# Two plain pairs of steps instead of three in both FFNs, with earlier squares and two low parts by accumulating DMA

## The chip, the cores and the metric

The kernel runs on one core of one Trainium2 chip. A core has a matrix engine (TensorE, PE in the profile; PEld is its weight loading), a vector engine (VectorE, DVE), a scalar engine (ScalarE, ACT), a general one (GpSimd, POOL) and a synchronising engine (SyncE, SP); each runs its own list of instructions in order and waits on semaphores for the others. DMA transfers are issued by an engine (here SP and POOL) and land later. The metric is the device time of one execution in microseconds (us).

## The reference

One sequence of 512 tokens with 1024 features goes through two layers, in fp32. Layer 0 is a dilated window attention, layer 1 an mLSTM; behind each stands a feed-forward network (FFN), and a final norm ends it. The change is in the two FFNs and in the norms ahead of them:

```python
def swiglu(xn, w_in, w_out):
    gu = xn @ w_in
    return (jax.nn.silu(gu[..., :D_FF]) * gu[..., D_FF:]) @ w_out
...
    for i in range(DEPTH):
        ...                       # h = h + mixer(rms_norm(h, ...))
        h = h + swiglu(rms_norm(h, ffn_norm[i]), ffn_w_in[i], ffn_w_out[i])
    return rms_norm(h, final_norm)
```

D_FF is 2816, so `w_in` is 1024x5632 per layer: the gate half and the up half.

## The kernel before, in words

Features lie on the 128 partitions, tokens along the free dimension: the residual stream is eight tiles h0 to h7 of 128x512. A product in fp32 precision is made of three matmuls in a shorter format (fp32r): each operand is split into a high part, a copy that ACT rounds, and a low part, the rest, which DVE subtracts; high by high, high by low and low by high are added up in PSUM (`SPLITS`, line 42). `split_chunk` (line 204) does this for a chunk of weights (128x1024, three buffers each for raw, high and low, `W_BUFS`), `split_act` and `x_tiles` for activations.

Ahead of an FFN, `norm` (line 828) splits h, scaled by the norm's gains, and makes the sum of squares: ACT squares each h tile, DVE adds it to `ssum`. PE sums over the partitions (tile n1ss in FFN 0, n3ss in FFN 1), DVE takes the reciprocal root, and `hook` (line 327) has PE spread it to all partitions, from where DVE copies it into `rbc`. The FFN's first matmuls don't wait for it: they multiply the unnormalised tokens, and `rbc` is applied to their result. The norm of FFN 0 (n1) stands behind the attention's output projection (`out_project`, tiles awo), which adds its result to h two tiles at a time; that of FFN 1 (n3) behind the mLSTM's (tiles mwo).

`ffn_in` (line 860) makes the hidden layer in 11 pairs of steps: pair j (j = 0, 2, ... 20) yields two blocks of 128 hidden features. The first PLAIN // 2 pairs, three here (`PLAIN`, line 857), are plain (`plain`, line 943): 96 matmuls of 128x512 through `multiply` (line 240), tiles f0j and f1j. At the end of a pair DVE multiplies four accumulators by `rbc` (tiles gu, line 959) and makes the hidden values (hid, line 964).

The other eight pairs use a scheme of seven products instead of eight (Strassen's, in Winograd's form). The weights of a pair are seen as blocks A11, A12, A21, A22 (half: gate or up; part: which 512 features of the input), the normalised tokens as B11, B12, B21, B22 (512 features by 256 tokens), and seven products of sums of them (`PRODUCTS`, S1 to S4 and T1 to T4) give the result. Each product is 24 matmuls of 128x256 (line 1017). The order is A11·B11, S1·T1, S2·T2, A12·B21, S3·T3, S4·B22, A22·T4; `products` (line 1005) writes them and reads their results, `weights_of` (line 970) loads the four blocks by SP (line 980), makes the sums S by DVE (line 988) and splits them, `AHEAD` = 2 products ahead.

The token operands are made once per FFN by the generator `normalized` (line 894), a few steps at a time beside the plain pairs: eight normalised tiles (f0x or f1x, line 900) into two buffers with the tag w8, x0 and x1 (x0 holds B11 and B12, x1 holds B21 and B22); T1 into a buffer with the tag t1 (tile f0t or f1t); T3 over B12, T2 over B22, T4 over B21. `split_tokens` (line 888) splits each of the seven into a high part (ACT, line 891) and a low part (DVE, line 892). The buffers are used again: the raw blocks A11 and A21 of the first seven-product pair go into x0's place, those of the second into x1's, and the sums S1, S2 of the first into t1's. So a first A11 load has to wait until all readers of B11, B12 and T3 are done, and the first S until those of T1 are.

In FFN 1, `residual` (line 1660) also turns h, two passes of transposes by DVE (hB) and transfers by POOL (hD) to device memory and back, for the natural token order at the end; in FFN 0 sums of hidden tiles (tile f0S) and of rows of the output weights (accumulating DMAs by POOL, line 1138) are made beside the pairs for the output stage, `output_products` (line 1090).

The order of each engine's instructions is fixed at build time: the statements are put in order by a scheduler that looks at dependences and buffers, so that an engine's list can differ from the order of the lines; it doesn't change at run time.

Of the kernel before, what the change touches and what calls it, by code (L numbers as in the profile page):

```python
# [11 lines left out]
F32 = mybir.dt.float32  # L12
F32R = mybir.dt.float32r
I32 = mybir.dt.int32
AF = mybir.ActivationFunctionType
ALU = mybir.AluOpType
AX = mybir.AxisListType
P = 128

SEQ = 512  # L20
D = 1024
KC = D // P
# [49 lines left out]
def tile_hybrid_dilated_attn_mlstm(  # L72
# [4 lines left out]
    nc = tc.nc  # L77
# [3 lines left out]
    def pool(stack, name, **kw):  # L81
        return stack.enter_context(tc.tile_pool(name=name, bufs=1, **kw))
# [147 lines left out]
    def x_tiles(name):  # L230
        parts = [xp.tile([P, 2, SEQ], F32R, tag="x%d" % i, name="%s_%s%d" % (name, "hl"[i % 2], i // 2))
                 for i in range(KC)]
        return [[parts[k // 2 * 2 + part][:, k % 2] for k in range(KC)] for part in range(2)]
# [11 lines left out]
    def project(pairs, w2d, c0, nk, evac, name, hook=None, ready=()):  # L245

        acc = [acc_tile("%s_%d" % (name, m)) for m in range(2)]
        for ch in range((nk + 3) // 4):
            n = min(4, nk - 4 * ch)
            whl = ready.pop(0) if ready else split_chunk(weight_chunk(w2d, ch, c0, n, "%s_k%d" % (name, ch)))  # L250
            for m in range(2):
                with fenced():
                    multiply(acc[m], whl, pairs, ch, m, nk)
                if 4 * ch + n == nk and hook is None:
                    evac(m, acc[m])
            if 4 * ch + n == nk and hook is not None:
                hook()
                for m in range(2):
                    evac(m, acc[m])
            advance()  # L260
# [81 lines left out]
    hp = pool(ctx, "h")  # L342
    npl = pool(ctx, "norm")
    h = [hp.tile([P, SEQ], F32, tag="h", name="h%d" % k, bufs=KC + 1) for k in range(KC)]

    with ExitStack() as actx:
        ap = pool(actx, "attn")
# [59 lines left out]
        pair = x_tiles("xa")  # L407
# [92 lines left out]
        rbc, rtok, bc_hook = inverse_rms(v, "x", box, then=lambda bp: rope_scale(bp))  # L500
# [28 lines left out]
        def rope_scale(bp):  # L529
            nc.vector.tensor_tensor(sinr, bp[:R], sinn, op=ALU.mult)  # L530
            nc.vector.tensor_tensor(rbc[:R], bp[:R], cosn, op=ALU.mult)
# [253 lines left out]
        pair = x_tiles("ao")  # L785
# [3 lines left out]
        def add_to_h(c):  # L789
            def evac(m, acc):  # L790
                nc.vector.tensor_tensor(h[2 * c + m], acc, h[2 * c + m], op=ALU.add)
            return evac

        def out_project(pairs, w2d, nk, name, first=0, end=KC // 2):
            for c in range(first, end):
                project(pairs, w2d, c * 256, nk, add_to_h(c), "%s%d" % (name, c))
# [7 lines left out]
        def out_part(c, whl, ch, ks=None, last=False):  # L804
            for m in range(2):
                with fenced():
                    multiply(acc[c][m], whl, pair, ch, m, KC, ks)
                if last:
                    add_to_h(c)(m, acc[c][m])
# [12 lines left out]
        for k in range(2, 4):  # L822
            for c in range(3):
                out_part(c, whl[c], 1, (k,), k == 3)
    out_project(pair, attn_w_out[0], KC, "awo", first=3)


    def norm(key, k0, name):
        pair = x_tiles(name)
        ssum = npl.tile([P, SEQ], F32, tag="ssum", name=name + "ssum")  # L830
        for k in range(KC):
            split_act(pair[0][k], pair[1][k], h[k], col(key, k0 + k))
            if k == 0:
                nc.scalar.activation(ssum, h[k], AF.Square)
            else:
                sq = npl.tile([P, SEQ], F32, tag="sq", name=name + "sq", bufs=2)
                nc.scalar.activation(sq, h[k], AF.Square)
                nc.vector.tensor_tensor(ssum, ssum, sq, op=ALU.add)
        v = npl.tile([P, TB], F32, tag="rs_v4", name=name + "v", bufs=2)
        box = {}  # L840

        def sums():
            sp = ps.tile([P, 512], F32, tag="t", name=name + "ss", bufs=1)
            for tb in range(TB):
                nc.tensor.matmul(sp[:, tb:tb + 1], ssum[:, tb * P:(tb + 1) * P], ones[:, 0:1],
                                 start=True, stop=True)
            nc.vector.tensor_copy(v, sp[:, :TB])
            box["finish"]()
        rbc, r, hook = inverse_rms(v, name, box)
        defer(1, sums)  # L850
        return pair, rbc, r, hook
# [2 lines left out]
    HALF = SEQ // 2  # L854

    PRODUCTS = (("A11", "B11"), ("S1", "T1"), ("S2", "T2"), ("A12", "B21"), ("S3", "T3"), ("S4", "B22"), ("A22", "T4"))
    PLAIN = 6
    AHEAD = 2

    def ffn_in(layer, fp, pair, rbc, hook, following, hid, during):  # L860
# [24 lines left out]

        ops, raw = {}, {}

        def split_tokens(key):
            i = [b for _, b in PRODUCTS].index(key)
            hi, lo = ops[key] = [op_tile(2 * i + part, key + "hl"[part]) for part in range(2)]  # L890
            nc.scalar.activation(hi, raw[key], AF.Copy)
            nc.vector.tensor_tensor(lo, raw[key], hi.bitcast(F32), op=ALU.subtract)

        def normalized():
            xs = [fp.tile([P, 4, SEQ], F32, tag="w8", name="f%dx%d" % (layer, i), bufs=2) for i in range(2)]
            for i in range(2):
                for t in range(2):
                    raw["B%d%d" % (i + 1, t + 1)] = xs[i][:, :, t * HALF:(t + 1) * HALF]
            for k in range(KC):
                nc.vector.scalar_tensor_tensor(xs[k // 4][:, k % 4], h[k], col("ffn", layer * KC + k), rbc,  # L900
                                               op0=ALU.mult, op1=ALU.mult)
                yield
            split_tokens("B11")
            raw["T1"] = fp.tile([P, 4, HALF], F32, tag="t1", name="f%dt1" % layer)
            nc.vector.tensor_tensor(raw["T1"], raw["B12"], raw["B11"], op=ALU.subtract)
            yield

            raw["T3"] = raw["B12"]
            nc.vector.tensor_tensor(raw["T3"], raw["B22"], raw["B12"], op=ALU.subtract)
            split_tokens("T1")  # L910
            yield
            split_tokens("T3")
            yield
            split_tokens("B22")
            yield
            raw["T2"] = raw["B22"]
            nc.vector.tensor_tensor(raw["T2"], raw["B22"], raw["T1"], op=ALU.subtract)
            split_tokens("T2")
            yield
            split_tokens("B21")  # L920
            yield

            raw["T4"] = raw["B21"]
            nc.vector.tensor_tensor(raw["T4"], raw["B21"], raw["T2"], op=ALU.subtract)
            split_tokens("T4")
# [4 lines left out]
        def some(n):  # L930
            for _ in itertools.islice(steps, n):
                pass


        chunks = [(j, ch, half) for j in range(0, PLAIN, 2) for ch in range(KC // 4) for half in range(2)]
        ready = []
# [126 lines left out]
        split_next()  # L1063
        for j in range(0, PLAIN, 2):
            plain(j)
        todo = [(j, i) for j in range(PLAIN, FC, 2) for i in range(len(PRODUCTS))]
        prepared = {}

        def prepare(n):
            if n < len(todo):  # L1070
                j, i = todo[n]
                if j not in prepared:
                    prepared[j] = weights_of(j)
                prepared[j][0][i]()
            else:
                following(n - len(todo))

        for n in range(AHEAD):
            prepare(n)
        some(None)  # L1080
        for n, (j, i) in enumerate(todo):
            prepare(n + AHEAD)
            if i == 0:
                steps_of = products(j, prepared[j][1])
            steps_of[i]()
            if i % 2:
                advance()
            during(j, i)
# [207 lines left out]
            return [(kind, ops[(a, b) if kind == "product" else b], whl[a, b]) for kind, a, b in items[-TAIL:]]  # L1296
        return hid, during, prepare, work

    pair, rbc, _, hook = norm("ffn", 0, "n1")
    with ExitStack() as fctx:  # L1300
        fp = pool(fctx, "ffn0")
        hid, during, prepare, work = output_products(0, fp, ffn_w_out[0], True)
# [24 lines left out]
        old, h = h, []  # L1327
# [26 lines left out]


    pair, rbc, rtok, hook = norm("mlstm", 0, "n2")
    w_in2 = mlstm_w_in[0]
    with ExitStack() as mctx:
# [138 lines left out]
        i = 0  # L1497
# [136 lines left out]
        ypair = x_tiles("yo")  # L1634
# [10 lines left out]
        run_deferred()  # L1645
        for j in range(H):
            split_act(ypair[0][j], ypair[1][j], y[j], hg[:, j:j + 1])
    out_project(ypair, mlstm_w_out[0], KC, "mwo")


    pair, rbc, _, hook = norm("ffn", KC, "n3")
    with ExitStack() as fctx:
        fp = pool(fctx, "ffn1")
        dp = pool(fctx, "scratch1", space=bass.MemoryType.DRAM)
# [11 lines left out]
                                    t[R * a_:R * (a_ + 1)])  # L1666

        def during(j, i):
            if i == 3:
                residual(((j - PLAIN) // 2 + 4) % KC)  # L1670
            operands(j, i)
        ffn_in(1, fp, pair, rbc, hook, prepare, hid, during)
# [131 lines left out]
```

## Time and profile before

| | us |
|---|---|
| median of 3 runs | 1409.27 |
| runs, lowest to highest | 1408.67 to 1409.78 |
| profiled execution, time | 1408.68 |
| profiled execution, span (first to last instruction) | 1406.9 |
| PE busy | 1394.5 |
| DVE busy | 1054.9 |
| ACT busy | 665.4 |
| POOL busy | 149.0 |

The times in the rows are counted from the span's start; FFN 0's first matmul starts at 503.20. A row of the timeline gives start and duration in us, engine, line, operation, and which tile is written from which; x2 stands for two such instructions in a row, and a bracket holds the idle time before it and what ended it. A duration includes time in which the next instruction of the engine has started, so the distance of two starts is the cost of one in a full queue.

### The profile page before, as it was taken

Reading aid. Unit: us, or ns where it says so; the run is one execution under the profiler, and the core shown is the slowest. Engines: PE = TensorE matmul, PEld = TensorE weight load, DVE = VectorE, ACT = ScalarE, POOL = GpSimd, SP = SyncE. Lnnn points to the kernel's source line nnn. Section 1 sums busy time; section 2 is a strip of 40 time slices with the busy share of each in tenths; the row PEclk is TensorE's granted clock in tenths of the full one; section 3 lists DMA queues with packets and bytes.
Section 4 is the critical chain, followed back from the end, with each engine's and each line's share of the span. In section 5 each row is a group of like instructions: output and inputs, shape, how many; then the busy total and the mean of one; then the engine's idle time right before and its main releaser. Section 6 shows DMA issues by size and latency. Waiting matters only on the chain. (4 is left out here: it accounts for less than half of the span.)

```text
span 1406.9 us, 21243 instructions
## 1 busy us (share of the span) xinstructions
PE 1394.5 (99%) x8226; PEld 1237.5 (88%) x8226; DVE 1054.9 (75%) x1832; ACT 665.4 (47%) x1111; POOL 149.0 (11%) x222
## 2 busy tenths in 40 slices
PE   9999999999999999999999999999999999999998
PEld 7888888888888888999999998888888899999886
DVE  7866557566567298777877898998758888887875
ACT  5333224224225253444576463786534444458744
POOL 1011011002002000000000101113101240001111
PEclk9999999999999999999999999999999999999999
DMA  6346245335434455433263733234333553335861
GB/s 195 102 109 203 76 117 160 118 106 131 159 105 121 157 143 156 106 120 119 68 180 85 161 110 103 82 89 106 96 100 105 168 158 117 120 102 125 174 192 60
DMA packets 137277, 176.02 MB, mean 125 GB/s; under 512 B 8596, under 2 KB 111316, under 8 KB 137176
## 3 DMA queue, kind: packets, MB, share of 16 engines
q1 hardware_dynamic: 121392, 134.17, 30.8%
q0 software_dynamic: 14128, 39.37, 12.5%
q8 instruction: 64, 1.05, 0.3%
q10 hardware_dynamic: 1656, 1.12, 0.2%
q14 instruction: 37, 0.30, 0.1%
HBM read 158.91 MB, written 15.73 MB: 124 GB/s over the span
## 5 line engine op out<-in xcount | busy, mean ns | idle before, releaser
L240 PE MATMUL f0j<-n_h,f0j_h 128*128 128x512 f32 x96 | 37.5, 390 | 0.0
L240 PE MATMUL f1j<-n_h,f1j_h 128*128 128x512 f32 x96 | 37.5, 390 | 0.0
L240 PE MATMUL f0j<-n_h,f0j_l 128*128 128x512 f32 x96 | 37.4, 389 | 0.0
L240 PE MATMUL f1j<-n_h,f1j_l 128*128 128x512 f32 x96 | 37.4, 389 | 0.0
L240 PE MATMUL f0j<-n_l,f0j_h 128*128 128x512 f32 x96 | 37.3, 389 | 0.0
L240 PE MATMUL f1j<-n_l,f1j_h 128*128 128x512 f32 x96 | 37.3, 389 | 0.0
L1138 POOL DMA_DIRECT2D f0S<-in_ffn_w_out_dram x10 | 8.7, 866 | 265.1 <-ACT f0P L1120 155.1
L1163 POOL DMA_DIRECT2D f1T<-in_ffn_w_out_dram x12 | 14.6, 1217 | 179.0 <-ACT f1T L1166 151.6
L1665 POOL DMA_DIRECT2D hD<-hB x32 | 20.7, 653 | 96.4 <-DVE hB L1662 96.4
L539 DVE TENSOR_TENSOR rot<-rot,sinr 32x1024 f32<-32x1024 f32 x24 | 28.9, 1206 | 0.0
L240 PE MATMUL mo<-n_h,mo_k_h 128*128 128x512 f32 x64 | 25.3, 396 | 0.0
L240 PE MATMUL mo<-n_h,mo_k_l 128*128 128x512 f32 x64 | 25.3, 395 | 0.0
L240 PE MATMUL mo<-n_l,mo_k_h 128*128 128x512 f32 x64 | 25.1, 393 | 0.0
L240 PE MATMUL mwo<-yo_l,mwo_k_h 128*128 128x512 f32 x64 | 25.1, 393 | 0.0
L240 PE MATMUL mqk<-n_h,mqk_k_h 128*128 128x512 f32 x64 | 25.1, 392 | 0.0
L240 PE MATMUL awo<-ao_h,awo_k_h 128*128 128x512 f32 x64 | 25.1, 392 | 0.0
L240 PE MATMUL mqk<-n_l,mqk_k_h 128*128 128x512 f32 x64 | 25.1, 392 | 0.0
L240 PE MATMUL mwo<-yo_h,mwo_k_l 128*128 128x512 f32 x64 | 25.0, 391 | 0.0
L240 PE MATMUL mqk<-n_h,mqk_k_l 128*128 128x512 f32 x64 | 25.0, 390 | 0.0
L240 PE MATMUL awo<-ao_h,awo_k_l 128*128 128x512 f32 x64 | 25.0, 390 | 0.0
L240 PE MATMUL awo<-ao_l,awo_k_h 128*128 128x512 f32 x64 | 24.9, 390 | 0.0
L240 PE MATMUL mwo<-yo_h,mwo_k_h 128*128 128x512 f32 x64 | 24.8, 391 | 0.0
(2282 smaller groups left out, 5461.3 us busy)
## 6 DMA issues: line engine op xcount, KB each, us to landing
f0j_w<-in_ffn_w_in_dram SPq DMA_DIRECT2D x28, 512.0 KB, 4.4
f1j_w<-in_ffn_w_in_dram SPq DMA_DIRECT2D x28, 512.0 KB, 4.9
f1T<-in_ffn_w_out_dram POOLq DMA_DIRECT2D x12, 512.0 KB, 7.1
awo_k_w<-in_attn_w_out_dram SPq DMA_DIRECT2D x8, 512.0 KB, 6.8
mv_k_w<-in_mlstm_w_in_dram SPq DMA_DIRECT2D x8, 512.0 KB, 3.7
mqk_k_w<-in_mlstm_w_in_dram SPq DMA_DIRECT2D x8, 512.0 KB, 3.7
mo_k_w<-in_mlstm_w_in_dram SPq DMA_DIRECT2D x8, 512.0 KB, 3.8
mwo_k_w<-in_mlstm_w_out_dram SPq DMA_DIRECT2D x8, 512.0 KB, 3.7
```

The costliest lines, as they stand in the source:

```text
L240: nc.tensor.matmul(acc, whl[a][:, k, m * P:(m + 1) * P], pairs[b][kk], start=(kk == 0 and (a, b) == SPLITS[0]), stop=(kk == nk - 1 and (a, ...
L539: nc.vector.tensor_tensor(sh, sh, sinr.unsqueeze(1).to_broadcast([R, 2, SEQ]), op=ALU.mult)
L1138: nc.gpsimd.dma_start(t, src[1][:, ks], accum_op=ALU.add)
L1163: nc.gpsimd.dma_start(view(to), weight_rows(hk * UNITS + u, n), accum_op=ALU.add)
L1665: nc.gpsimd.dma_start(hD[k // 4].rearrange("(b i) x -> i b x", i=R)[:, :, c0:c0 + R], t[R * a_:R * (a_ + 1)])
```

## The change

- `PLAIN` goes from 6 to 4: each FFN has two plain pairs and nine seven-product pairs.
- The squares and their sum are made by a function of their own, `squares_of`, ahead of the norm: in FFN 0 those of h0 to h5 before the last tile pair of the output projection, in FFN 1 two at a time inside the loop of the output projection.
- The low parts of B11 and T1 are no longer subtracted by DVE: ACT writes minus the high part into the low tile, and a DMA issued by POOL adds the raw tile to it.
- T1's split comes before T3 is made; one step of `normalized` is taken ahead of the first weights and one at each product, where all that were left were taken at once.
- `residual` runs for the first eight seven-product pairs only, since there are nine.

```diff
--- before.py
+++ after.py
@@ -342,6 +342,19 @@
     hp = pool(ctx, "h")
     npl = pool(ctx, "norm")
     h = [hp.tile([P, SEQ], F32, tag="h", name="h%d" % k, bufs=KC + 1) for k in range(KC)]
+
+    def squares_of(name):
+
+        ssum = npl.tile([P, SEQ], F32, tag="ssum", name=name + "ssum")
+
+        def add(k):
+            if k == 0:
+                nc.scalar.activation(ssum, h[k], AF.Square)
+            else:
+                sq = npl.tile([P, SEQ], F32, tag="sq", name=name + "sq", bufs=2)
+                nc.scalar.activation(sq, h[k], AF.Square)
+                nc.vector.tensor_tensor(ssum, ssum, sq, op=ALU.add)
+        return ssum, add
 
     with ExitStack() as actx:
         ap = pool(actx, "attn")
@@ -822,20 +835,24 @@
         for k in range(2, 4):
             for c in range(3):
                 out_part(c, whl[c], 1, (k,), k == 3)
+
+    ssum, add_square = squares_of("n1")
+    for k in range(KC - 2):
+        add_square(k)
     out_project(pair, attn_w_out[0], KC, "awo", first=3)
-
-
-    def norm(key, k0, name):
+    for k in range(KC - 2, KC):
+        add_square(k)
+
+
+    def norm(key, k0, name, ssum=None):
         pair = x_tiles(name)
-        ssum = npl.tile([P, SEQ], F32, tag="ssum", name=name + "ssum")
+        add = None
+        if ssum is None:
+            ssum, add = squares_of(name)
         for k in range(KC):
             split_act(pair[0][k], pair[1][k], h[k], col(key, k0 + k))
-            if k == 0:
-                nc.scalar.activation(ssum, h[k], AF.Square)
-            else:
-                sq = npl.tile([P, SEQ], F32, tag="sq", name=name + "sq", bufs=2)
-                nc.scalar.activation(sq, h[k], AF.Square)
-                nc.vector.tensor_tensor(ssum, ssum, sq, op=ALU.add)
+            if add is not None:
+                add(k)
         v = npl.tile([P, TB], F32, tag="rs_v4", name=name + "v", bufs=2)
         box = {}
 
@@ -854,7 +871,7 @@
     HALF = SEQ // 2
 
     PRODUCTS = (("A11", "B11"), ("S1", "T1"), ("S2", "T2"), ("A12", "B21"), ("S3", "T3"), ("S4", "B22"), ("A22", "T4"))
-    PLAIN = 6
+    PLAIN = 4
     AHEAD = 2
 
     def ffn_in(layer, fp, pair, rbc, hook, following, hid, during):
@@ -885,11 +902,16 @@
 
         ops, raw = {}, {}
 
-        def split_tokens(key):
+        def split_tokens(key, by_dma=False):
+
             i = [b for _, b in PRODUCTS].index(key)
             hi, lo = ops[key] = [op_tile(2 * i + part, key + "hl"[part]) for part in range(2)]
             nc.scalar.activation(hi, raw[key], AF.Copy)
-            nc.vector.tensor_tensor(lo, raw[key], hi.bitcast(F32), op=ALU.subtract)
+            if by_dma:
+                nc.scalar.activation(lo, hi.bitcast(F32), AF.Copy, scale=-1.0)
+                nc.gpsimd.dma_start(lo, raw[key], accum_op=ALU.add)
+            else:
+                nc.vector.tensor_tensor(lo, raw[key], hi.bitcast(F32), op=ALU.subtract)
 
         def normalized():
             xs = [fp.tile([P, 4, SEQ], F32, tag="w8", name="f%dx%d" % (layer, i), bufs=2) for i in range(2)]
@@ -900,14 +922,14 @@
                 nc.vector.scalar_tensor_tensor(xs[k // 4][:, k % 4], h[k], col("ffn", layer * KC + k), rbc,
                                                op0=ALU.mult, op1=ALU.mult)
                 yield
-            split_tokens("B11")
+            split_tokens("B11", True)
             raw["T1"] = fp.tile([P, 4, HALF], F32, tag="t1", name="f%dt1" % layer)
             nc.vector.tensor_tensor(raw["T1"], raw["B12"], raw["B11"], op=ALU.subtract)
             yield
 
+            split_tokens("T1", True)
             raw["T3"] = raw["B12"]
             nc.vector.tensor_tensor(raw["T3"], raw["B22"], raw["B12"], op=ALU.subtract)
-            split_tokens("T1")
             yield
             split_tokens("T3")
             yield
@@ -917,6 +939,7 @@
             nc.vector.tensor_tensor(raw["T2"], raw["B22"], raw["T1"], op=ALU.subtract)
             split_tokens("T2")
             yield
+
             split_tokens("B21")
             yield
 
@@ -1075,10 +1098,11 @@
             else:
                 following(n - len(todo))
 
+        some(1)
         for n in range(AHEAD):
             prepare(n)
-        some(None)
         for n, (j, i) in enumerate(todo):
+            some(1)
             prepare(n + AHEAD)
             if i == 0:
                 steps_of = products(j, prepared[j][1])
@@ -1296,7 +1320,7 @@
             return [(kind, ops[(a, b) if kind == "product" else b], whl[a, b]) for kind, a, b in items[-TAIL:]]
         return hid, during, prepare, work
 
-    pair, rbc, _, hook = norm("ffn", 0, "n1")
+    pair, rbc, _, hook = norm("ffn", 0, "n1", ssum)
     with ExitStack() as fctx:
         fp = pool(fctx, "ffn0")
         hid, during, prepare, work = output_products(0, fp, ffn_w_out[0], True)
@@ -1645,10 +1669,14 @@
         run_deferred()
         for j in range(H):
             split_act(ypair[0][j], ypair[1][j], y[j], hg[:, j:j + 1])
-    out_project(ypair, mlstm_w_out[0], KC, "mwo")
-
-
-    pair, rbc, _, hook = norm("ffn", KC, "n3")
+    ssum, add_square = squares_of("n3")
+    for c in range(KC // 2):
+        out_project(ypair, mlstm_w_out[0], KC, "mwo", c, c + 1)
+        add_square(2 * c)
+        add_square(2 * c + 1)
+
+
+    pair, rbc, _, hook = norm("ffn", KC, "n3", ssum)
     with ExitStack() as fctx:
         fp = pool(fctx, "ffn1")
         dp = pool(fctx, "scratch1", space=bass.MemoryType.DRAM)
@@ -1666,7 +1694,7 @@
                                     t[R * a_:R * (a_ + 1)])
 
         def during(j, i):
-            if i == 3:
+            if i == 3 and (j - PLAIN) // 2 < KC:
                 residual(((j - PLAIN) // 2 + 4) % KC)
             operands(j, i)
         ffn_in(1, fp, pair, rbc, hook, prepare, hid, during)
```

## Prediction

> **What bounds the kernel now.** I read the page, the cores, and then the waits of TensorE (columns: total us, times, longest).
>
> ```profile
> span 1406.9 us, 21243 instructions
> PE 1394.5 (99%) x8226; PEld 1237.5 (88%) x8226; DVE 1054.9 (75%) x1832; ACT 665.4 (47%) x1111; POOL 149.0 (11%) x222
> core 0: 1406.9 us, clock 0.999
> PE idle L108 <- DVE idle_w L103: 1.5, 1, 1.5
> PE m2num L1575 <- DVE m1yt L1596: 1.3, 1, 1.3
> ...
> PE m6yT L306 <- DVE m6yt L1596: 0.2, 1, 0.2
> ```
>
> PE works 99% of the span at full clock. All eight places where it waits are listed in that view, 0.2 to 1.5 us each, and none is in ffn_in. There only matmul time can be saved; any wait for an operand is new loss. Stage by stage, and in the chain:
>
> ```profile
> 526.00:548.00 22.00, 22.00 (x99) 18.22 (x98) 21.92 (x25) 11.43 (x12) 0.28 (x1) 1.00 0.58 166
> 570.00:590.00 20.00, 20.00 (x169) 20.00 (x168) 15.66 (x16) 9.83 (x12) 2.59 (x3) 1.00 0.73 186
> 1085.00:1107.00 22.00, 22.00 (x99) 18.22 (x98) 21.95 (x25) 10.16 (x11) 0.00 (x0) 1.00 0.47 147
> 1107.00:1129.00 22.00, 22.00 (x99) 18.22 (x98) 15.71 (x20) 6.35 (x7) 7.75 (x12) 1.00 0.56 152
> 1129.00:1149.00 20.00, 20.00 (x168) 19.92 (x167) 16.34 (x19) 9.87 (x12) 9.91 (x17) 1.00 0.66 180
> 1077.78 51.70 PE f1j L240 x228
> 1132.36 2.88 PE f1j_p L1017 x24
> ```
>
> Window columns: busy us of PE, PEld, DVE, ACT, POOL, then clock, DMA share, GB/s. PE is full throughout. DVE is full too (21.92 and 21.95 of 22) in the second plain pair, where it makes the token operands; in the third it has slack (15.71), and in seven-product pairs (15.66, 16.34 of 20). The change removes that third pair, DVE's catch-up time.
>
> **The gain.** 228 plain matmuls take 51.70, 226.8 ns each; a plain pair of 96 takes 21.77 us. A seven-product pair is 7 products of 24 matmuls at 2.88: 20.16 us. One swap saves 1.61 us per FFN, 3.22 in both. As PE waits nowhere here, that is the ceiling.
>
> **When the first seven-product operands come.** The rows of DVE in FFN 1 (start, duration, then line and tile):
>
> ```profile
> 1090.33 1.22 DVE L892 TENSOR_TENSOR f1B11l<-f1x,f1B11h 128x1024 fp32r<-128x1024 f32 x1
> 1091.47 1.22 DVE L905 TENSOR_TENSOR f1t<-f1x 128x1024 f32<-128x1024 f32 x1
> 1094.87 1.22 DVE L892 TENSOR_TENSOR f1T1l<-f1t,f1T1h 128x1024 fp32r<-128x1024 f32 x1
> ...
> 1097.14 1.22 DVE L892 TENSOR_TENSOR f1T3l<-f1x,f1T3h 128x1024 fp32r<-128x1024 f32 x1
> ...
> 1100.55 0.69 DVE L959 TENSOR_TENSOR f1j2gu<-f1j,n3rbc 128x512 f32<-128x512 f32 x1
> 1101.15 1.21 DVE L892 TENSOR_TENSOR f1B21l<-f1x,f1B21h 128x1024 fp32r<-128x1024 f32 x1
> ...
> 1112.38 0.70 DVE L1662 STREAM_TRANSPOSE hB<-hn 128x512 f32<-128x512 f32 x1
> 1113.01 1.18 DVE L988 TENSOR_TENSOR f1j_w<-f1j_w 128x1024 f32<-128x1024 f32 x1
> 1098.50 0.37 SPq L980 DMA_DIRECT2D f1j_w<-in_ffn_w_in_dram  x1
> 1118.46 1.06 ACT L209 ACTIVATE f1j6A_h<-f1j_w 128x1024 fp32r<-128x1024 f32 x1 [4.38 <-PE f1j L240]
> 1119.56 1.22 DVE L210 TENSOR_TENSOR f1j6A_l<-f1j_w,f1j6A_h 128x1024 fp32r<-128x1024 f32 x1 [3.59 <-ACT f1j6A_h L209]
> 1129.32 0.28 PE L1017 MATMUL f1j_c<-f1B11h,f1j6A_h 128*128 128x256 f32 x1
> DMA to landing us min/median/max: 3.4/4.9/6.8
> DMA to landing us min/median/max: 3.5/4.4/6.5
> ```
>
> Starts 1090.33 and 1091.47 give a pitch of 1.135 us for a 128x1024 operation; 0.60 for a 128x512 one (1100.55 to 1101.15), 0.63 for a transpose. A weight's low part starts 1.10 after ACT's high part; with its first 0.05, 1.15 after landing. The landing rows are for the weight loads of FFN 1 and FFN 0.
>
> The two A11/A21 loads of a first seven-product pair go into the buffer of x0, so they are issued once T3l, the last reader, is done: before, at 1098.36, and SP issued at 1098.50. After, DVE's order from the last normalised tile on is: t1 at 1090.33, transpose, T3, one plain low part, B22l, B21l, then T3l at 1096.63 (5×1.135+0.63 later), done at 1097.85. Issue about 1098.0, half a microsecond earlier, while PE now needs the products 21.77 us earlier.
>
> FFN 1 on from there, with the median landing 4.9: A11's low part starts at 1098.0+4.9+1.15=1104.05. DVE then holds, in order, A11l, S, gu, S3, hid, gu, S1l, hid, S2, T4l, transpose, S2l: 6×1.135 + 4×0.60 + 0.63 + 1.22 = 11.06, so S2l ends at 1115.1. The first seven-product matmul started at 1129.32; after, it can start at 1129.32−21.77=1107.55. Products one and two last 5.76, so the third (S2 by T2) can start at 1113.31 and wants the low part a matmul pitch later (two of 0.12), 1113.55. Stall about 1.55 us. With landing 3.5 DVE itself is the limit (T2, transpose, gu, T2l, T4, gu lie before A11l) and 0.15 remains; with 6.8 it is 3.45. S1l ends near 1110.5 for a need at 1110.67: next to no margin.
>
> FFN 0 by the same steps:
>
> ```profile
> 530.60 1.22 DVE L892 TENSOR_TENSOR f0B11l<-f0x,f0B11h 128x1024 fp32r<-128x1024 f32 x1
> ...
> 539.68 1.22 DVE L892 TENSOR_TENSOR f0T3l<-f0x,f0T3h 128x1024 fp32r<-128x1024 f32 x1
> 569.93 0.28 PE L1017 MATMUL f0j_c<-f0B11h,f0j6A_h 128*128 128x256 f32 x1
> ```
>
> Here t1 takes B11l's place at 530.60, and then come a 128x512 sum, T3, B22l and a plain low part, so T3l moves up from 539.68 to 530.60+4×1.135+0.60=535.74 and ends at 536.96: loads at 537.1, A11l at 537.1+4.4+1.15=542.65. Twelve operations, 6×1.135+5×0.60+1.22=11.03, end with S2l at 553.7. The first product can start at 569.93−21.77=548.16, the third wants S2l at 548.16+6.0=554.16: no stall, 0.4 to spare. With 6.5 it is 1.6.
>
> **The accumulating DMAs.** B11l and T1l leave DVE (2×1.135 per FFN, counted above), and ACT gets two copies each near 1.06 per FFN, beside 11.43 and 10.16 of 22: hidden; without that cover, 2.1 us per FFN. SBUF to SBUF accumulation is not in the trace. Nearest are accumulating loads from HBM, 512 KB likewise (their issue on POOL, the landing of that line, and of FFN 0's), and 64 KB moves out of SBUF:
>
> ```profile
> L1163 POOL DMA_DIRECT2D f1T<-in_ffn_w_out_dram x12 | 14.6, 1217 | 179.0 <-ACT f1T L1166 151.6
> DMA to landing us min/median/max: 5.9/7.3/9.6
> f0T<-in_ffn_w_out_dram POOLq DMA_DIRECT2D x5, 512.0 KB, 8.6
> hD<-hB POOLq DMA_DIRECT2D x32, 64.0 KB, 3.4
> ```
>
> Bounds 3.4 to 9.6; I take 7.3, of the same size and kind. B11l's DMA goes out near 526.3 in FFN 0 and is needed, for the A11 load, at 536.9: slack 10.6. T1l's goes out near 536.7, and S, which takes T1's buffer, is to start at 544.5: slack 7.8 (9.7 in FFN 1: 1095.5 to 1105.2). Cost 0 at 7.3; at 9.6 FFN 0 stalls 9.6−8.2=1.4, as the third product's spare 0.4 comes first. What is queued behind the waiting S on DVE is gu and S1l, and behind these PE. In POOL's queue these DMAs stand between hD transfers of transposes 5 to 7, which are done by 1092.8; nothing urgent waits behind them.
>
> The Trainium skill, "SBUF — State Buffer", section "Who interferes with whom", has a rule against this: a software-generated DMA can stall while DVE holds the port it shares with GpSimd. By it T1l's DMA, sent while DVE is full, would be late, and the sum be that of the slower rival below. The rows from FFN 0's output stage show the like beside a busy DVE:
>
> ```profile
> 781.00:802.00 21.00, 21.00 (x156) 20.04 (x155) 19.02 (x25) 9.05 (x10) 5.42 (x5) 1.00 0.76 161
> ```
>
> Five of them with DVE at 19.02 of 21 landed at 8.6 median, 1.3 above the whole line's, so I leave it as a chance.
>
> **Squares and the rest.** Sixteen squares and 14 sums are moved, none added. In FFN 0 the sums are needed by
>
> ```profile
> 501.94 1.22 DVE L210 TENSOR_TENSOR f0j_l<-f0j_w,f0j_h 128x1024 fp32r<-128x1024 f32 x1
> 508.64 0.95 PE L845 MATMUL n1ss<-ones,n1ssum 128*128 128x1 f32 x8
> ```
>
> which has a fixed place in PE's order, so finishing the sums early gains nothing. A weight's low part moves from 501.94 to about 507.3–508.5, needed at 509.1: cost 0, at 0.6 us margin; if that is gone, about 1. In FFN 1 the order barely changes: 0. On SP the A22 and A12 loads come ahead of A11, into buffers long free: 0. The guarded residual never runs twice: 0. These zeros have no gain side, since PE waits for none of it.
>
> **Sum.** −3.22 + 1.55 + 0 = −1.67. The profiled execution took 1408.68 (span 1406.9 and 1.78 around it), 0.59 below the median 1409.27: 1407.0 on its own scale, 1407.6 on the median's. Landing bounds of the weight loads alone: −3.22+0.15 = −3.1 to −3.22+3.45+1.6 = +1.8; a DMA at 9.6 beside them is inside that.
>
> **Rivals.** *Everything is in time.* Weight loads land in 3.5, as the shortest do: −3.2 to −3.1, 1406.1 to 1406.2. For it: window 1085 to 1107 has a DMA share of only 0.47. Against: DVE has no free microsecond there.
>
> *T1l's DMA lands late (slower).* SBUF is read and written for every element; S waits, with S1l, S2l and PE behind it, in both FFNs. With landing L the stalls are (L−8.2) + (1.55+L−9.7). They reach 6.0, which is +2.8 net, at L = 11.2; at L = 13 they are 9.65, +6.4, 1415.7. For it: 9.6 is measured, in the trace, 1.6 short of the point. Against: medians of 7.3 and 8.6.
>
> *The clock drops after a stall.* Row: at the span's start
>
> ```profile
> L108 PE MATMUL idle<-idle_w,ones_r 128*128 128x512 f32 x14 | 5.4, 542 | 1.5 <-DVE idle_w L103 1.5
> L240 PE MATMUL f1j<-n_h,f1j_h 128*128 128x512 f32 x96 | 37.5, 390 | 0.0
> 952.00:957.00 5.00, 5.00 (x40) 4.63 (x39) 4.52 (x11) 3.09 (x11) 2.94 (x4) 1.00 0.30 43
> ```
>
> 14 matmuls took 542 ns where later ones take 390: 14×0.152=2.1 us, giving −1.67+2.1=+0.4, 1409.7. But after the 1.3 us wait at m2num the clock was 1.00. The Trainium skill, "TensorE: Matmul & The Clock Gate", section "Part 1: The HAM clock gate (the “warmup” mystery)", puts the limit at about 3.4 us idle, which agrees.
>
> That the change doesn't do what it says is excluded: PE's order has 168 matmuls in place of 96 in each FFN.
>
> **How the numbers follow.** Forecast 0.45, all in time 0.28, late DMA 0.23, clock 0.04. A change under 0.2% (2.8 us) is about what a measurement of this kernel can't tell from none. Faster needs nearly the whole ceiling: most of the second case and the forecast's tail, 0.30. Slower is most of the third and a tail of the forecast for rows my bounds miss, 0.23; same 0.47. Forecast 1407.6; its own range is 1406.2 to 1411.1 by the landing bounds (−3.1 to +1.8 about 1409.27). The range for 8 in 10 runs from 1405.9 (−3.2 less run scatter) to 1412.1 (+2.8, where the late DMA begins to tell).
>
> **What would show it.** Right: the first seven-product matmul of each FFN 21.8 us earlier against its stage's start, with DVE's windows before it as full as now; the waits gain one place in FFN 1, f1j_u of the first seven-product pair on DVE's low part of S2, 1 to 2 us, and none in FFN 0; the ffn_in stage is 1.6 us shorter in FFN 0 and nearly unchanged in FFN 1. Wrong: no such row (second case); waits at S with a DMA of T1l as releaser, or landings of that line over 11 us (third); a clock under 1.00 behind the stall (fourth); a wait at n1ss or f0j0's last chunk would break the squares' zero.

## The result: 2.75 us slower, where 1.7 us less was forecast

The changed kernel takes 1411.64 us (median of 21 runs, 1411.05 to 1413.17), the kernel before beside it 1408.89 us. The ratio is 1.0018 (95% interval 1.0012 to 1.0024): 2.75 us slower. The time lies inside the stated range, but the forecast had the sign wrong. The profiled execution took 1411.64 us. One execution among the experiments below, of the kernel a11_t4, ran at a granted clock of 0.75 and took 2502.91 us; it is left out of that kernel's ratio.

The page after:

```profile
span 1409.9 us, 21577 instructions
PE 1393.7 (99%) x8370; PEld 1243.1 (88%) x8370; DVE 1063.9 (75%) x1838; ACT 677.8 (48%) x1127; POOL 153.5 (11%) x226
```

PE's waits after, those that are new (columns as before: total us, times, longest):

```profile
PE f1j_p L1040 <- DVE f1j4S_l L210: 1.3, 1, 1.3
PE f0j_u L1040 <- ACT f0j_u L1052: 1.1, 1, 1.1
PE f0j_u L1040 <- DVE f0j4S_l L210: 0.7, 1, 0.7
PE f1j_c L1040 <- ACT f1j4A_h L209: 0.4, 1, 0.4
PE f1j_u L1040 <- DVE f1j4S_l L210: 0.3, 1, 0.3
```

Five waits are new, all in the first seven-product pair of an FFN. Their sum, 3.8, is too small, as the ends of matmuls are modelled; starts of products don't have that fault. From the first product on S1 to the product that ends the disturbed stretch:

```profile
551.82 0.28 PE L1040 MATMUL f0j_p<-f0T1h,f0j4S_h 128*128 128x256 f32 x1
560.04 0.28 PE L1040 MATMUL f0j_c<-f0B21h,f0j4A_h 128*128 128x256 f32 x1
1111.99 0.28 PE L1040 MATMUL f1j_p<-f1T1h,f1j4S_h 128*128 128x256 f32 x1
1123.65 0.28 PE L1040 MATMUL f1j_u<-f1T3h,f1j4S_h 128*128 128x256 f32 x1
```

FFN 0: two products in 8.22 us, where 2 x 2.88 = 5.76 is the undisturbed time: 2.46 lost. FFN 1: three in 11.66 against 8.64: 3.02 lost. All other products of both stages start 2.88 apart as before, and each FFN saves its 1.61. So −3.22 + 5.48 = +2.3 us, which accounts for the measured 2.75 within its interval (1.7 to 3.4). The two profiled executions are 2.96 apart: there another 0.77 is lost in the first 12 us (PE's second group of xT starts at 12.15 where it started at 11.38), ahead of anything that the change touches.

How the loss comes about, in rows of SP, POOL, ACT and DVE, first FFN 0, then FFN 1:

```profile
536.47 1.22 DVE L914 TENSOR_TENSOR f0T3l<-f0x,f0T3h 128x1024 fp32r<-128x1024 f32 x1
537.55 0.88 POOL L912 DMA_DIRECT2D f0T1l<-f0t  x1 [9.59 <-ACT f0T1l L911]
537.76 13.49 SPq L1003 DMA_DIRECT2D f0j_w<-in_ffn_w_in_dram  x4
545.11 1.06 ACT L209 ACTIVATE f0j4A_h<-f0j_w 128x1024 fp32r<-128x1024 f32 x1 [5.19 <-DMA f0j_w<-in_ffn_w_in_dram]
546.21 1.23 DVE L210 TENSOR_TENSOR f0j4A_l<-f0j_w,f0j4A_h 128x1024 fp32r<-128x1024 f32 x1 [3.29 <-ACT f0j4A_h L209]
556.02 1.22 DVE L210 TENSOR_TENSOR f0j4S_l<-f0j4S,f0j4S_h 128x1024 fp32r<-128x1024 f32 x1
...
1097.15 0.94 POOL L912 DMA_DIRECT2D f1T1l<-f1t  x1 [1.85 <-ACT f1T1l L911]
1097.75 1.70 POOL L1693 DMA_DIRECT2D hD<-hB  x2
1098.15 1.22 DVE L914 TENSOR_TENSOR f1T3l<-f1x,f1T3h 128x1024 fp32r<-128x1024 f32 x1
1099.51 21.99 SPq L1003 DMA_DIRECT2D f1j_w<-in_ffn_w_in_dram  x6
1101.42 2.58 POOL L1693 DMA_DIRECT2D hD<-hB  x4 [1.97 <-DVE hB L1690]
1106.10 1.06 ACT L209 ACTIVATE f1j4A_h<-f1j_w 128x1024 fp32r<-128x1024 f32 x1 [3.59 <-DMA f1j_w<-in_ffn_w_in_dram]
1107.19 1.23 DVE L210 TENSOR_TENSOR f1j4A_l<-f1j_w,f1j4A_h 128x1024 fp32r<-128x1024 f32 x1 [2.47 <-ACT f1j4A_h L209]
1117.04 1.19 DVE L210 TENSOR_TENSOR f1j4S_l<-f1j4S,f1j4S_h 128x1024 fp32r<-128x1024 f32 x1
```

From the issue of the first A11 load (the start of the SP row) to ACT's use of it, for which ACT waited by the bracket, pass 545.11−537.76 = 7.35 us and 1106.10−1099.51 = 6.59 us. The forecast had 4.4 and 4.9. DVE, full until then, stands idle in front of A11's low part, for 3.29 us in FFN 0 and 2.47 in FFN 1.

What the DMA engines do while the first weight loads are on their way, after and then before (last columns: clock, DMA share, GB/s):

```profile
540.00:543.00 3.00, 3.00 (x15) 2.49 (x14) 2.92 (x3) 0.00 (x0) 0.00 (x0) 1.00 1.08 238
1099.50:1103.00 3.50, 3.50 (x18) 2.88 (x16) 3.47 (x5) 1.70 (x2) 1.58 (x3) 1.00 1.05 152
```

```profile
540.00:543.00 3.00, 3.00 (x15) 2.48 (x14) 3.00 (x4) 0.88 (x2) 0.00 (x0) 1.00 0.63 185
1099.50:1103.00 3.50, 3.50 (x17) 2.91 (x16) 3.50 (x5) 2.33 (x3) 0.00 (x0) 1.00 0.80 257
```

After the change they are full (1.08 and 1.05); before they weren't (0.63, where the loads go out only from 539.8 to 541.4, and 0.80 with three loads on their way). New among the transfers is T1's accumulating DMA, sent 0.2 us ahead of the loads in FFN 0 and 2.4 us ahead in FFN 1. In FFN 1 six moves of transposed tiles (hD, 64 KB each) run there too, which the kernel before makes at other times; in FFN 0 there are none.

### The profile page after: what moved, and what is told of

It reads as the page before. It is cut to its first block, busy times and chain, and to the rows that moved or that the text cites. A ratio compares the mean times of both kernels' runs of the same rounds, so it can differ in the third digit from the quotient of the medians.

```text
span 1409.9 us, 21577 instructions
## 1 busy us (share of the span) xinstructions
PE 1393.7 (99%) x8370; PEld 1243.1 (88%) x8370; DVE 1063.9 (75%) x1838; ACT 677.8 (48%) x1127; POOL 153.5 (11%) x226
## 3 DMA queue, kind: packets, MB, share of 16 engines
q8 instruction: 66, 1.08, 0.3%
## 5 line engine op out<-in xcount | busy, mean ns | idle before, releaser
L240 PE MATMUL f0j<-n_h,f0j_h 128*128 128x512 f32 x64 | 25.0, 391 | 0.0
L240 PE MATMUL f1j<-n_h,f1j_h 128*128 128x512 f32 x64 | 25.0, 391 | 0.0
L240 PE MATMUL f1j<-n_h,f1j_l 128*128 128x512 f32 x64 | 25.0, 390 | 0.0
L240 PE MATMUL f0j<-n_h,f0j_l 128*128 128x512 f32 x64 | 24.9, 390 | 0.0
L240 PE MATMUL f0j<-n_l,f0j_h 128*128 128x512 f32 x64 | 24.9, 389 | 0.0
L240 PE MATMUL f1j<-n_l,f1j_h 128*128 128x512 f32 x64 | 24.9, 389 | 0.0
```

The costliest lines, as they stand in the source:

```text
L240: nc.tensor.matmul(acc, whl[a][:, k, m * P:(m + 1) * P], pairs[b][kk], start=(kk == 0 and (a, b) == SPLITS[0]), stop=(kk == nk - 1 and (a, ...
```

## The experiments

Theory A: T1's accumulating DMA shares the DMA engines with the A11 and A21 loads and makes them late; S, S1 and S2 come late behind them. Rival B: the weight loads, sent out together, slow each other, with or without that DMA.

**A quarter of T1's DMA.**

```diff
-                nc.gpsimd.dma_start(lo, raw[key], accum_op=ALU.add)
+                part = slice(0, 1) if key == "T1" else slice(0, 4)
+                nc.gpsimd.dma_start(lo[:, part], raw[key][:, part], accum_op=ALU.add)
```

> The changed kernel, but T1's accumulating DMA moves only the first of its four feature blocks (128 KB instead of 512 KB); the other three blocks of T1's low part keep minus the high part, so that part of the computation is left out. Order of all engines unchanged. Theory A (that DMA slows the A11 and A21 loads issued beside it): the first A11 load of FFN 0 lands in about 5 us instead of 7.3, that of FFN 1 in about 5 to 5.5 instead of 6.5; the stalls of the first seven-product pairs fall from 2.46 and 3.02 us to 0 to 0.3 and 1.5 to 2, the time by 3 to 4 us, to about 1 us below the kernel before. Theory B (the three weight loads issued together slow each other): landings of 7.3 and 6.5, stalls and time as in the changed kernel, +2.7 against before.

Measured: 1409.00 us beside 1409.24 before, ratio 0.9998 (0.9990 to 1.0007).

```profile
538.01 12.22 SPq L1004 DMA_DIRECT2D f0j_w<-in_ffn_w_in_dram  x4
544.10 1.06 ACT L209 ACTIVATE f0j4A_h<-f0j_w 128x1024 fp32r<-128x1024 f32 x1 [3.93 <-DMA f0j_w<-in_ffn_w_in_dram]
1098.63 20.91 SPq L1004 DMA_DIRECT2D f1j_w<-in_ffn_w_in_dram  x6
1104.08 1.06 ACT L209 ACTIVATE f1j4A_h<-f1j_w 128x1024 fp32r<-128x1024 f32 x1 [2.44 <-DMA f1j_w<-in_ffn_w_in_dram]
```

The loads land after 6.09 and 5.45 us, and the first pairs lose 1.18 and 1.86 us by the starts of their products, 3.04 instead of 5.48. The ratio lies clear of the changed kernel's (1.0012 to 1.0024). B is out as the whole cause: nothing but the size of that DMA differs, and the hD moves of FFN 1 are there as before. Yet FFN 0 lost more than A had expected (1.18 against 0 to 0.3).

**T1's low part by DVE.**

```diff
-            split_tokens("T1", True)
+            split_tokens("T1")
```

> The changed kernel, but T1's low part is subtracted by DVE as before; B11's still by DMA. T3's low part then ends 1.1 us later in FFN 0 and 1.1 us earlier in FFN 1 (DVE order), and T2's low part comes behind A11's in FFN 1. Theory A: landings near 5 without the DMA, stalls of 1.0 and 2.2 us, together 3.2: the gain of 3.2 is just used up, the time about that of before (0 to +0.8). Theory B: landings of 7.3 and 6.5, stalls 3.4 and 3.7, +4 against before.

Measured: 1410.10 beside 1409.24, ratio 1.0009 (1.0000 to 1.0017).

```profile
538.73 0.92 SPq L1003 DMA_DIRECT2D f0j_w<-in_ffn_w_in_dram  x2
542.97 1.06 ACT L209 ACTIVATE f0j4A_h<-f0j_w 128x1024 fp32r<-128x1024 f32 x1 [0.77 <-DMA f0j_w<-in_ffn_w_in_dram]
1098.17 21.34 SPq L1003 DMA_DIRECT2D f1j_w<-in_ffn_w_in_dram  x6
1102.35 1.06 ACT L209 ACTIVATE f1j4A_h<-f1j_w 128x1024 fp32r<-128x1024 f32 x1 [5.70 <-DMA f1j_w<-in_ffn_w_in_dram]
```

Its windows at the places where the changed kernel's engines were full:

```profile
540.00:543.00 3.00, 3.00 (x15) 2.49 (x14) 3.00 (x4) 1.56 (x3) 0.00 (x0) 1.00 0.99 302
1099.50:1103.00 3.50, 3.50 (x17) 2.90 (x16) 3.50 (x4) 0.65 (x1) 0.00 (x0) 1.00 0.91 291
```

From issue to use A11 takes 4.24 and 4.18 us without the DMA. The engines move 302 GB/s at a share of 0.99 in FFN 0, where with T1's DMA they moved 238 at 1.08. In FFN 1 it is 291 at 0.91 against 152 at 1.05, but there the hD moves have gone from beside the loads as well: they are issued by 1096, ahead of them. The stall in FFN 1 falls from 3.02 to 1.21. In FFN 0 the third product loses only 0.55, but 1.7 us are lost in the same pair further on: there DVE stood 4.1 us in front of the second pair's S. Three loads for the output stage had come ahead of that pair's w8 loads in SP's queue, which is the likely reason; the profile names no releaser. The sum of 3.5 is near the 3.2 expected, its places are not.

**Two plain pairs, and nothing else of the change.**

```diff
-    PLAIN = 6
+    PLAIN = 4
...
-            if i == 3:
+            if i == 3 and (j - PLAIN) // 2 < KC:
```

> The kernel before with two plain pairs instead of three and the guard on the ninth residual, nothing else of the change. T3's low part ends 2 us later than in the changed kernel in FFN 0 and 0.5 us later in FFN 1, and no accumulating DMA runs beside the loads. Theory A: landings of 4.5 to 5, stalls of about 2.4 and 2.5, together 4.9, +1.7 against before. Theory B: landings of 6.5 to 7, stalls near 4.5 and 4, +5 against before. In both the rest of the change is worth little.

Measured: 1409.86 beside 1409.24, ratio 1.0003 (0.9994 to 1.0012).

```profile
540.65 10.20 SPq L980 DMA_DIRECT2D f0j_w<-in_ffn_w_in_dram  x4
544.71 1.06 ACT L209 ACTIVATE f0j4A_h<-f0j_w 128x1024 fp32r<-128x1024 f32 x1 [1.73 <-DMA f0j_w<-in_ffn_w_in_dram]
```

Landings of 4.06 and, in FFN 1, 4.02: the fastest yet, though the A11 and A21 loads go out together as always. First pairs lose 1.77 and 1.53, so −3.22 + 3.30 = +0.1. The swap alone is nearly neutral, and what was added to help it cost 2.2 us of stalls more.

**Everything of the change but the swap.**

```diff
-    PLAIN = 4
+    PLAIN = 6
```

> The changed kernel with three plain pairs again: early squares, two low parts by DMA, new order of the operand steps, guard. All that the change does beside the swap of a pair. By the prediction's zeros: no wait of PE in either FFN, within 0.5 us of the kernel before. If instead 0.5 to 1 us more is lost, it is in the squares or in the longer program.

Measured: 1409.54 beside 1409.13, ratio 1.0002 (0.9994 to 1.0011). No wait of PE in either FFN, all products 2.88 apart: squares, copies by ACT and DMAs cost nothing where a third plain pair covers them.

**Both low parts by DVE.** `split_tokens("B11")` and `split_tokens("T1")`, both without the DMA.

> The changed kernel with both low parts (B11 and T1) subtracted by DVE again; squares, order and the two plain pairs as changed. Theory A: A11 landings of about 4.1 us as without T1's DMA; DVE has 2.3 us more per FFN ahead of the loads; stalls of 3 to 4 us together, 0 to +1 against before, that is 1.5 to 2.5 us better than the changed kernel: the two DMAs cost more than they save. Rival: the DMAs are worth their DVE time, and this one is slower than the changed kernel.

Measured: 1410.25 beside 1409.13, ratio 1.0008 (0.9999 to 1.0016); stalls of 2.94 and 1.04, 4.0 together. As expected by A, though the intervals of the two kernels' ratios just overlap: the two DMAs cost more than the 2.3 us of DVE per FFN that they save, as long as the loads run beside one of them. That one is T1's: in the kernel with T1's low part by DVE and B11's by DMA the stalls were 3.5.

**A11 into a buffer that is free early.** If A11's landing is what counts, it need not share T3's buffer: A12, wanted only by the fourth product, can.

```diff
-            w = {"A11": w8[:, 0], "A21": w8[:, 1]}
-            for key in ("A22", "A12"):
+            w = {"A12": w8[:, 0], "A21": w8[:, 1]}
+            for key in ("A11", "A22"):
...
-            for key in ("A11", "A22", "A12", "A21"):
+            for key in ("A11", "A22", "A21", "A12"):
```

> The changed kernel with the places of two raw weight blocks exchanged: A11 goes into a buffer of the weight ring (free early), A12 into the w8 buffer that has to wait for T3's low part, and the loads go out in the order A11, A22, A21, A12. A11 is then there in time; the first sum S has to wait for A21, about 2.2 us of DVE and ACT work later than A11 was wanted. Both theories: the wait of ACT for the first A11 is gone; with A21 landing 7.3 and 6.5 after its issue the last S2 low part ends about 553 in FFN 0 and 1114.5 in FFN 1, before PE wants it (554.9 and 1115.1): stalls 0 to 0.5 together, the time 2 to 3 us below the kernel before. If stalls of 2 us or more stay, the landing of the first A11 load is not what set them.

Measured: 1409.22 beside 1409.24, ratio 1.0006 (0.9996 to 1.0016); its runs scatter from 1408.30 to 1415.40, and the profiled execution, at 1414.18, is one of the three above 1413. The 2 to 3 us that were expected did not come. In that execution the first three products run undisturbed in both FFNs, as expected, but the rest of the pair doesn't. PE's longest wait:

```profile
PE f0j_u L1040 <- DVE f0j4v L1046: 4.6, 1, 4.6
```

SP and DVE ahead of that wait:

```profile
557.81 5.50 SPq L1003 DMA_DIRECT2D f0j_w<-in_ffn_w_in_dram  x4
566.84 1.23 DVE L1011 TENSOR_TENSOR f0j6S<-f0j_w,f0j6A 128x1024 f32<-128x1024 f32 x1 [5.48 <-DMA f0j_w<-in_ffn_w_in_dram]
```

With A11 out of the way the scheduler had put T4 behind the weight sums. The second pair's w8 loads wait for T4's low part, so they went out at 557.81, behind three loads for the output stage, and took 9.0 us to their use; DVE stood 5.48 us for them in front of the second S, with PE's results queued behind it. This trace is of a late execution: what held the other eight runs, whose times are about those of the kernel before, isn't shown by it.

**A11 early, and T4 early too.** The edit above, and all remaining operand steps before the first weights:

```diff
-        some(1)
+        some(None)
         for n in range(AHEAD):
             prepare(n)
```

> The kernel with A11 and A12 exchanged, and all steps of the token operands written before the first weights, so that T4 and its low part come ahead of the later weight sums on DVE and the w8 loads of the second seven-product pair (which wait for T4's low part) go out some 10 us earlier, ahead of three loads for the output stage in SP's queue. Theory A with its second step (first A11's landing, then the second pair's w8 loads): no stall in FFN 0, 0 to 0.5 us in FFN 1 at the third product; 2.5 to 3.2 us below the kernel before. If the second pair still stalls by 2 us or more, its loads are not what held it.

Measured: 1406.67 beside 1409.13, ratio 0.9983 (0.9974 to 0.9992). The same kernel a second time:

> The same kernel as the one that exchanges A11 and A12 and makes the token operands' last step early, run again, since the profile left of it is of an execution at a clock of 0.75. By theory A its trace shows A21 landing 6 to 7.5 us after its issue with T1's DMA beside it, no wait of PE in FFN 0's first seven-product pair and at most 0.5 us in FFN 1's, and a time 2 to 3 us below the kernel before, as the first time (2.46).

Measured: 1407.24 beside 1409.25, ratio 0.9984 (0.9975 to 0.9992).

PE's one new wait:

```profile
PE f1j_u L1040 <- DVE f1j8S_l L210: 1.0, 1, 1.0
```

POOL, DVE and PE around the first pairs, and DVE ahead of that wait:

```profile
537.48 0.88 POOL L912 DMA_DIRECT2D f0T1l<-f0t  x1 [9.33 <-ACT f0T1l L911]
545.31 1.22 DVE L1011 TENSOR_TENSOR f0j4S<-f0j_w,f0j4A 128x1024 f32<-128x1024 f32 x1 [0.80 <-DMA f0T1l<-f0t]
548.89 0.28 PE L1040 MATMUL f0j_c<-f0B11h,f0j4A_h 128*128 128x256 f32 x1
569.04 0.28 PE L1040 MATMUL f0j_c<-f0B11h,f0j6A_h 128*128 128x256 f32 x1
1106.70 0.28 PE L1040 MATMUL f1j_c<-f1B11h,f1j4A_h 128*128 128x256 f32 x1
1126.85 0.28 PE L1040 MATMUL f1j_c<-f1B11h,f1j6A_h 128*128 128x256 f32 x1
...
1156.26 1.23 DVE L1011 TENSOR_TENSOR f1j10S<-f1j_w,f1j10A 128x1024 f32<-128x1024 f32 x1 [2.67 <-DMA f1j10A<-in_ffn_w_in_dram]
```

Both first pairs take 20.15 us, no stall at all. One of 1.26 us by the starts is new in FFN 1, in the third seven-product pair, where DVE had stood 2.67 us for a load of the fourth: −3.22 + 1.26 = −1.96, measured −2.0. This kernel beats both others, by 2.0 to 2.5 us the kernel before and by 4.4 to 5 us the changed one.

**T4 early alone.** The last edit without the exchange of A11 and A12.

> The changed kernel with only the early operand steps (T4 and its low part ahead of the weight sums), A11 and A12 where the change has them. Theory A: the first A11 still lands 6.5 to 7.5 us after its issue, beside T1's DMA; S stands behind T4's low part on DVE, so S1's low part is about 1 us later than in the changed kernel and the stalls are as large or larger, 5 to 7 us together: +2 to +3.5 against before. If this one is also 2 us below the kernel before, the order of T4 and not the place of A11 was the cure.

Measured: 1412.90 beside 1409.25, ratio 1.0029 (1.0017 to 1.0040). A11 lands 7.37 and 6.46 us after its issue, the first pairs lose 3.44 and 2.97. So neither edit alone was the cure: moving T4 alone makes it worse, moving A11 alone left the median where it was.

**Exchange, T4 early, and no DMA for the low parts.**

> The exchange of A11 and A12 with all operand steps early, and no accumulating DMA for low parts: DVE has 2.3 us more work per FFN ahead of the first products, A21 lands in about 4 us. Theory A: stalls of 1 to 1.5 us in FFN 0 and 1 to 2 in FFN 1, between -1 and +0.3 against before: with the load out of the way DVE itself is the limit, and the DMAs are worth about 2 us. If it equals the one with the DMAs, DVE's time is not what remains.

Measured: 1410.19 beside 1409.13, ratio 1.0008 (0.9999 to 1.0017): 1.15 us lost in FFN 0, as expected, but 2.94 and, two pairs on, 0.96 in FFN 1, 2 us more than expected. It is 3 to 3.5 us slower than with the DMAs: once no urgent load runs beside them they are worth their traffic. DVE has no idle time over 0.6 us around the stalls of the two first pairs, so its time is what limits there; ahead of the 0.96 it stood 2.36 us for a load, as the kernel with the DMAs did at the same place.

## Why the prediction was wrong, point by point

- *The ceiling* held: the plain stage is 21.76 us shorter in each FFN, the products 2.88 us each, the gain 3.22.
- *When the operands come* held to a tenth. T3's low part was put at 535.74 and 1096.63; the profiled execution runs 0.78 us late by then in FFN 0 and 1.55 in FFN 1, and shows 536.47 and 1098.15.
- *The landing of the A11 load* is the step that failed, and with it the 0 that the sum had for the accumulating DMAs: 4.4 and 4.9 assumed, 7.35 and 6.59 measured, and in FFN 0 more than the longest that it had allowed for (6.5). With these lateness terms (2.95 and 1.7, of which 2.8 and 1.6 reach DVE) the prediction's own chain gives the end of S2's low part as 553.7+0.78+2.8 = 557.3 and 1115.1+1.55+1.6 = 1118.25; the trace has 557.24 and 1118.23. So the chain was right and one of its terms was mis-sized, by enough to turn the sign: 2.46 of stall in FFN 0 for 0, 3.02 in FFN 1 for 1.55. In FFN 1 the larger part of it comes already at S1, whose low part the prediction had ready at 1110.5 with next to no margin; it ends at 1113.63, again 1.55 and 1.6 later.
- Why it was mis-sized: the new DMA was weighed only by when it lands itself, not by what it takes from the loads beside it. Without it, A11 took 4.0 to 4.2 us in two experiments, less than either median, so the median of the tile was no bad price for these loads by themselves. The trace of before suggests that the loads slow each other too (B has a part): there a load for the last plain pair goes out between A11 and A21, and the landing row of FFN 1's weight loads in the window 1098 to 1102, which has no landing of A11 but those of the other two, reads

```profile
DMA to landing us min/median/max: 5.8/6.3/6.8
```

  With two loads and no other transfer, in the kernel with the swap alone, A21 landed in 4.9. That row was within reach of the prediction and would have warned that a load takes longer among others. What the six hD moves add to the 6.59 of FFN 1 no experiment separates; the prediction asked what waits behind them in POOL's queue, not which loads run beside them.
- *The accumulating DMAs.* Their own landings lie inside the bounds of 3.4 to 9.6: in the trace after, 7.3 and 7.7 us for B11 and T1 in FFN 0, 5.8 and 5.7 in FFN 1. S did not wait for T1's; DVE was still waiting for A11. The slower rival had the right culprit, the right sign and the wrong way: T1's DMA never reached the 11.2 us, and hurt the loads beside it, not by being late itself. That it does so by the DMA engines' time is read from their share (1.08 and 1.05); no run separates that from another resource that the transfers share.
- *The Trainium skill's rule* on GpSimd's shared port ("SBUF — State Buffer", "Who interferes with whom") isn't shown at work here, and no run excludes it: POOL's issue of T1's DMA took 0.88 us beside a full DVE. The same section of the Trainium skill says that `tensor_tensor`, which is nearly all that DVE ran then, was not seen to stall a DMA, so the prediction stretched the rule.
- *The zeros* for squares, copies and order held together: the kernel with three plain pairs and all the rest has no new wait and is +0.4 us, within its interval.
- *The clock* stayed at 0.999, with waits of up to 1.3 us on PE.
- *All in time* (0.28) was not this change; the exchange of two buffers with T4 early comes within 1.3 us of it.
- *The range* held by luck: 1411.64 is inside it because its top was set by a T1 DMA that lands late, which isn't what happened; the forecast's own range ended at 1411.1.

## What to carry to other kernels

When work is moved to the DMA engines, price it twice: by when it lands, and by what it does to the loads that fly with it. Here the second price decided: in FFN 0 T1's DMA landed in time and still made the A11 load some 3 us late (7.35 against 4.1 to 4.2). A median over loads without the new transfer can't hold that price; the landing among other transfers, in the window where the load is wanted, comes closer. Ask what else is on the way when the new transfer starts. And where a load is late because of whose buffer it inherits, exchanging it with a block that is wanted later may gain more than moving work; look then for the next load that becomes the last to arrive, as here that of the second pair.

## What the runs showed of the hardware

From its issue to its use, the first A11 load of 512 KB took, in FFN 0, 4.1 us with no SBUF-to-SBUF accumulation beside it (4.2 in another kernel), 6.1 with one of 128 KB and 7.35 with one of 512 KB. A quarter of the bytes did over half of the harm; why is open, as the number of packets wasn't varied apart from the bytes. In FFN 1 the numbers are 4.0 (4.2), 5.5 and 6.6, but there the kernels with the accumulation have six hD moves beside the loads too, and the 128 KB had landed 0.8 us after the first load went out. While the larger accumulation ran in FFN 0 the DMA engines were busier than without it (1.08 against 0.99) and moved less (238 against 302 GB/s).
